# Linear attention: sixteen rows of the output per partition in place of eight, and a second matmul in four blocks of 32 columns

## The chip, the cores and the metric

The kernel runs on one core of a Trainium2 chip. The metric is the device time of one execution in microseconds (us), and the number to forecast is the median of several executions. Before the change the median of three is 126.47 us (126.22 to 126.54).

The names used below: PE is TensorE, which multiplies matrices; PEld is its weight load; DVE is VectorE; ACT is ScalarE; POOL is GpSimd, which here clears a few buffers and issues most of the DMAs; SP is SyncE, which only issues DMAs. SBUF is the on-chip memory of 128 partitions, PSUM the memory that TensorE writes into, DRAM the memory in which inputs and outputs lie.

## The reference

Q, K and V are float32 arrays of 8 x 12 heads, 512 rows and 64 columns. For each of the 96 heads:

```python
Q_feat = np.maximum(0, Q) + 1
K_feat = np.maximum(0, K) + 1
KV = np.einsum('bhkd,bhkv->bhdv', K_feat, V)            # 64 x 64 for a head
K_sum = np.sum(K_feat, axis=2)                          # 64 for a head
numerator = np.einsum('bhqd,bhdv->bhqv', Q_feat, KV)    # 512 x 64
denominator = np.einsum('bhqd,bhd->bhq', Q_feat, K_sum)
out = numerator / (denominator[:, :, :, None] + 1e-10)
```

That is 12.58 MB for each of Q, K, V and the output. The kernel leaves the 1e-10 out, since the denominator is a sum of products that are all at least 1.

## The kernel before

**Heads and groups.** The 96 heads go in twelve groups of eight heads (`NG` = 12), and two groups form a pair `s`, six pairs in all. A DMA load takes a whole pair of one input (1024 KB in SBUF as bf16; POOL's DMAs convert from float32 on the way), except at the start, where K and V come in halves and the first half of Q comes as float32 over SP's queue. K and V are seen as blocks of 128 partitions x 16 rows, so a partition reads 4 KB in one piece from DRAM and a head lies on 32 partitions. Q is seen as blocks of 128 partitions x 32 rows (8 KB in one piece), so a head lies on 16 partitions.

**First matmul.** `k_features` (L150) computes max(x + 1, 1) on DVE. `v_blocks` (L157) copies V into a block-diagonal buffer `v_all`, three of its four 32-partition blocks on DVE (L164) and one on ACT (L162). `keys_values` (L175) then does 32 matmuls of 64 result columns x 260 moving columns a group, with K_sum as an extra column for each head, and ACT moves the result to `kva` (L190, L191), one of `NV` = 4 buffers by group.

**Transposes.** `q_features` (L168) does the same max for Q; `transposes` (L193) turns it with 16 matmuls against an identity, into two PSUM tiles of 1024 columns, and ACT copies each (L204; one of them DVE) to `qt`, in which the columns stand by row-in-block `c`, partition and chunk `r`.

**Second matmul.** `out_matmuls(g, h)` (L206) takes from `qt` 16 partitions x R = 4 chunks, which are 64 columns and so 64 rows of the result, against the 130 columns of a pair of heads in `kva` (numerator and denominator of two heads). Two such blocks (`j`) fill the 128 partitions of PSUM, and eight `c` fill two tiles `o_ps` of two banks each: 16 matmuls a call, two calls a group, 384 in all. `norms` (L223) then takes for each tile a reciprocal of the denominators (L231) and one multiply of 128 x 512 (L232) into `o_sb`. An output partition holds `C` = 8 consecutive rows, which is 2 KB of DRAM. Only two tiles `o_ps` exist, so TensorE refills one while DVE empties the other.

**Order.** The order of the instructions on each engine is the order of the program (`tc.manual_schedule`, L256). In the loop (L275), group `g` is loaded, featured and multiplied while `output(g - 2)` is done two groups later. `load_pair(s + 2)` (L126) is issued by POOL as soon as DVE and ACT have read the buffers of pair `s` (`in_pool` has two of each). No store is issued until all loads are: from `g == NG - 5` on (L290) POOL issues the stores of the groups that are done, one of 1024 KB for each group, and the last two groups are stored over SP's queue, group 10 with one DMA (L138) and group 11 with two halves (L141), of which each takes what one call of `norms(11, h)` has written.

Of the kernel before, what the change touches and what calls it, by code (L numbers as in the profile page):

```python
# [8 lines left out]
FP32 = mybir.dt.float32  # L9
BF16 = mybir.dt.bfloat16  # L10
# [9 lines left out]
def kernel(  # L20
# [19 lines left out]
    nc = tc.nc  # L40

    B, H, S, D = Q.shape
    P = 128
    C = 8
    C2 = 2 * C
    C4 = 4 * C
    R = 4
    NPAIR = B * H * S // (P * C)
    NP = 4
    NG = NPAIR // NP  # L50
    D1 = D + 1
    W = 2 * D1

    def view(t, c):
        return t.flatten_outer_dims().rearrange("(n p c) d -> p n c d", p=P, c=c)

    q_eights = view(Q, C4)
    k_dram = view(K, C2)
    v_dram = view(V, C2)
    o_dram = view(out, C)  # L60

    const = ctx.enter_context(tc.tile_pool(name="const", bufs=1))
    in_pool = ctx.enter_context(tc.tile_pool(name="in_pool", bufs=IN_BUFS))
    kf_pool = ctx.enter_context(tc.tile_pool(name="kf_pool", bufs=2))
    qf_pool = ctx.enter_context(tc.tile_pool(name="qf_pool", bufs=3))
    mid_pool = ctx.enter_context(tc.tile_pool(name="mid", bufs=2))
    out_pool = ctx.enter_context(tc.tile_pool(name="out_pool", bufs=OUT_BUFS))
# [3 lines left out]
    psum_qt = ctx.enter_context(tc.tile_pool(name="psum_qt", bufs=2, space=bass.MemoryType.PSUM))  # L71

    identity = const.tile([P, P], BF16, name="identity")
    NV = 4
    v_all = const.tile([P, 2, 2, C2, 4 * D1], BF16, name="v_all")
    ones = const.tile([P, 4], BF16, name="ones")
    zero = const.tile([P, 1], FP32, name="zero")
    kva_all = const.tile([P, NV, 4, 2, D1], BF16, name="kva_all")
    kva_diag = [kva_all[:, i] for i in range(NV)]

    drams = dict(k=k_dram, v=v_dram)
    raw = {}
    bufs = {}
    kfs = {}
    qfs = {}
    qts = {}
    outs = {}
    cells_of = {}

    def load_first_q():  # L90
        t = out_pool.tile([P, 2 * NP, C, D], FP32, name="o_sb")
        half = t[:, 0:NP].rearrange("p n c d -> p (n c) d")
        nc.sync.dma_start(out=half, in_=q_eights[:, 0])
        return half

    def load_rest_q(t):
        u = in_pool.tile([P, 2, C4, D], BF16, name="q_raw")
        nc.gpsimd.dma_start(out=u[:, 1], in_=q_eights[:, 1])
        for e in range(2):
            raw["q", e] = [  # L100
                x.rearrange("p (r c) d -> p r c d", c=C)[:, :, 4 * e : 4 * e + 4]
                for x in (t, u[:, 1])
            ]

    def load(x, groups):
        s = groups[0] // 2
        if groups[0] % 2 == 0 or (x, s) not in bufs:
            bufs[x, s] = in_pool.tile([P, 4, C2, D], BF16, name=f"{x}_raw")
        if len(groups) == 2:
            ms = slice(0, 4)  # L110
            of = slice(4 * s, 4 * s + 4)
        else:
            ms = slice(groups[0] % 2, 4, 2)
            of = slice(4 * s + groups[0] % 2, 4 * s + 4, 2)
        nc.gpsimd.dma_start(out=bufs[x, s][:, ms], in_=drams[x][:, of])  # L115
        for g in groups:
            raw[x, g] = bufs[x, s][:, g % 2 : 4 : 2]

    def load_q(s):
        t = in_pool.tile([P, 2, C4, D], BF16, name="q_raw")  # L120
        nc.gpsimd.dma_start(out=t, in_=q_eights[:, 2 * s : 2 * s + 2])  # L121
        rows = t.rearrange("p n (r c) d -> p n r c d", c=C)
        for e in range(2):
            raw["q", 2 * s + e] = [rows[:, n, :, 4 * e : 4 * e + 4] for n in range(2)]

    def load_pair(s):  # L126
        load("k", (2 * s, 2 * s + 1))
# [1 line left out]
        load_q(s)  # L129

    def store(g):
        s = g // 2
        o_to = o_dram[:, 2 * NP * s : 2 * NP * s + 2 * NP]
        if g < NG - 2:
            nc.gpsimd.dma_start(out=o_to[:, g % 2 : 2 * NP : 2], in_=outs[s][:, g % 2 : 2 * NP : 2])  # L135
            return
        if g == NG - 2:
            nc.sync.dma_start(out=o_to[:, 0 : 2 * NP : 2], in_=outs[s][:, 0 : 2 * NP : 2])  # L138
            return
        for h in range(2):  # L140
            nc.sync.dma_start(  # L141
                out=o_to[:, 2 * h + g % 2 : 2 * NP : NP], in_=outs[s][:, 2 * h + g % 2 : 2 * NP : NP]
            )

    def feature(dst, src):
        nc.vector.tensor_scalar(  # L146
# [2 lines left out]

    def k_features(g):  # L150
        k_raw = raw.pop(("k", g))
        kf = kf_pool.tile([P, C2, 2, D], BF16, name="kf")
        for n in range(2):
            feature(kf[:, :, n], k_raw[:, n])
        kfs[g] = kf
# [12 lines left out]
    def q_features(g):  # L168
        q_raw = raw.pop(("q", g))
        qf = qf_pool.tile([P, R, C // 2, 2, D], BF16, name="qf")  # L170
        for n in range(2):
# [3 lines left out]
    def keys_values(g):  # L175
        kf = kfs.pop(g)
        kva_ps = psum_kva.tile([P, 4 * D1], FP32, name="kva_ps")
        for c in range(C2):
            for n in range(2):
                nc.tensor.matmul(  # L180
                    kva_ps[64 * n : 64 * n + 64],
                    lhsT=kf[:, c, n, :],
                    rhs=v_all[:, g % 2, n, c, :],
                    start=(c == 0),
                    stop=(c == C2 - 1),
                )
        kva = kva_diag[g % NV]
        for n in range(2):
            ps = slice(64 * n, 64 * n + 64)
            nc.scalar.copy(out=kva[ps, :, n, 0:D], in_=kva_ps[ps, 0 : 4 * D].rearrange("p (b d) -> p b d", b=4))  # L190
            nc.scalar.copy(out=kva[ps, :, n, D], in_=kva_ps[ps, 4 * D : 4 * D1])  # L191

    def transposes(g):  # L193
        qf = qfs.pop(g)
        if g % 2 == 0:
            qts[g // 2] = mid_pool.tile([P, C, P, R], BF16, name="qt")
        for half in range(2):
            qt_ps = psum_qt.tile([P, 2, R, P], BF16, name="qt_ps")
            for c in range(2):
                for r in range(R):  # L200
                    nc.tensor.transpose(qt_ps[:, c, r], qf[:, r, 2 * half + c, :, :], identity)  # L201
            copy = nc.vector.tensor_copy if half and g == NG - 2 else nc.scalar.copy
            lo = g % 2 * 4 + 2 * half
            copy(out=qts[g // 2][:, lo : lo + 2], in_=qt_ps.rearrange("p c r q -> p c q r"))  # L204

    def out_matmuls(g, h):  # L206
        qt = qts[g // 2]
        kva = kva_diag[(g // 2 * 2 + h) % NV]
        ops = [psum.tile([P, 2, BANK], FP32, tag="ps", name="o_ps") for _ in range(2)]
        for c in range(C):  # L210
            for j in range(2):
                b = 2 * (g % 2) + j
                q = 16 * (4 * h + b)
                nc.tensor.matmul(  # L214
                    ops[c // 4][64 * j : 64 * j + 64, c // 2 % 2, (c % 2) * W : (c % 2) * W + W],
                    lhsT=qt[:, c, q : q + 16, :],
                    rhs=kva[:, b],
                    start=True,
                    stop=True,
                )  # L220
        cells_of[g, h] = ops

    def norms(g, h):  # L223
        ops = cells_of.pop((g, h))
        if (g % 2, h) == (0, 0):
            outs[g // 2] = out_pool.tile([P, 2 * NP, C, D], FP32, name="o_sb")
        o_sb = outs[g // 2]
        for i in range(2):
            cells = ops[i][:, :, 0 : 2 * W].rearrange("p b (c n x) -> p b c n x", n=2, x=D1)
            recip = recip_pool.tile([P, 2, 2, 2, 1], FP32, name="recip")  # L230
            nc.vector.reciprocal(out=recip, in_=cells[:, :, :, :, D:D1])  # L231
            nc.vector.tensor_tensor(  # L232
                out=o_sb[:, 2 * h + g % 2 : 2 * NP : NP, 4 * i : 4 * i + 4].rearrange(
                    "p n (b c) d -> p b c n d", b=2
                ),
                in0=cells[:, :, :, :, 0:D],
                in1=recip.to_broadcast([P, 2, 2, 2, D]),
                op=ALU.mult,
            )

    def output(g):
        for h in range(2):
            out_matmuls(g, h)
            norms(g, h)

    def clear(i):
        t = v_all[:, i].rearrange("p n c x -> p (n c x)").bitcast(FP32)
        w = t.shape[1] * 5 // 8
        nc.vector.memset(t[:, 0:w], 0.0)  # L249
        nc.scalar.copy(out=t[:, w:], in_=zero.to_broadcast([P, t.shape[1] - w]))  # L250
        nc.vector.tensor_copy(
            out=v_all[:, i, :, :, 4 * D : 4 * D1].rearrange("p n c j -> p (n c) j"),
            in_=ones[:, None, :].to_broadcast([P, 2 * C2, 4]),
        )

    with tc.manual_schedule():  # L256
# [16 lines left out]
        clear(1)  # L273
        last = NG - 1
        for g in range(last - 1):  # L275
# [11 lines left out]
            keys_values(g)  # L287
            if g % 2 and g // 2 + 2 < NG // 2:
                load_pair(g // 2 + 2)
# [55 lines left out]
```

## Time and profile before

| what | us |
|---|---|
| median of the runs | 126.47 |
| the profiled execution, its own time | 126.1 |
| span of that execution, first to last instruction | 124.3 |
| DVE busy in it | 89.6 |
| TensorE matmuls busy | 63.5 |
| ACT busy | 59.6 |
| last instruction of DVE ends | 113.5 |

The 1.8 us between the span and the execution's own time lie before the first and after the last instruction. The profile cuts the span into 40 slices of 3.1 us and gives for each the busy share of each engine in tenths, the granted TensorE clock, the mean busy share of the 16 DMA engines and what they moved. The rate in GB/s counts the bytes as they stand in SBUF, so a load that converts float32 to bf16 moves twice the shown rate on the DRAM side, and a store just the shown rate. A window is a stretch of the span with the same figures. A share above 1 means that a DMA engine had more than one packet in work.

### The profile page before, as it was taken

How to read it: one execution, taken by the hardware profiler on the slowest of the kernel's cores; microseconds unless marked ns; L12 is line 12 of the kernel's file. 1: busy time of each engine (PE TensorE's matmuls, PEld its weight loads, DVE VectorE, ACT ScalarE, POOL GpSimd, SP SyncE). 2: the span in 40 equal slices, each digit the busy share in tenths (PEclk: the TensorE clock that was granted, in tenths of full speed). 3: DMA queues.
4: the chain of work that ended last, by engine and by line, in shares of the span. 5: the costliest groups of instructions: out<-in, count | busy, mean ns of one | idle time of the engine just before them, and what ended most of it. 6: DMA issues, size and time to landing. Idle time of an engine off the chain costs nothing.

```text
span 124.3 us, 2346 instructions
## 1 busy us (share of the span) xinstructions
PE 63.5 (51%) x960; PEld 52.0 (42%) x960; DVE 89.6 (72%) x190; ACT 59.6 (48%) x86; POOL 25.7 (21%) x53
## 2 busy tenths in 40 slices
PE   0000864500593837629775494928964888652000
PEld 0000754400482737418664383816742757521000
DVE  4885744206999989997999989999169999695000
ACT  7505079606019881866539568393577065300000
POOL 6992021200001400222002392202202200200000
PEclk9999999965579999995899769995596579985555
DMA  3999999999999999999999999999999999999994
GB/s 90 327 211 217 205 208 212 214 214 213 208 211 212 215 223 204 211 213 219 209 212 212 213 215 210 216 208 216 219 287 420 420 419 416 406 415 416 415 409 155
DMA packets 11819, 32.13 MB, mean 258 GB/s; under 512 B 544, under 2 KB 544, under 8 KB 11680
## 3 DMA queue, kind: packets, MB, share of 16 engines
q0 software_dynamic: 10592, 28.84, 97.6%
q1 hardware_dynamic: 1216, 3.15, 6.7%
q8 instruction: 7, 0.11, 0.3%
q14 instruction: 4, 0.03, 0.1%
HBM read 37.75 MB, written 12.58 MB: 405 GB/s over the span
## 4 chain that ended last, share of the span: by engine, by line
DMA 40%; DVE 29%; PE 12%; ACT 7%; issue 2%; POOL 1%; POOLq 0%
DMA v_raw<-in_V_dram 40%; DVE o_sb L232 12%; DVE v_all L164 10%; PE kva_ps L180 8%; ACT qt L204 3%; ACT v_all L162 3%; PE qt_ps L201 3%; DVE recip L231 3%; DVE qf L146 2%; DVE kf L146 1%; PE o_ps L214 1%; DVE qt L204 1%; POOL k_raw L115 1%; ACT kva_all L190 1%; ACT kva_all L191 0%
## 5 line engine op out<-in xcount | busy, mean ns | idle before, releaser
L180 PE MATMUL kva_ps<-v_all,kf 128*64 128x260 bf16 x384 | 30.8, 327 | 15.8 <-DVE v_all L164 14.1
L214 PE MATMUL o_ps<-kva_all,qt 128*64 128x130 bf16 x384 | 20.0, 240 | 31.4 <-DVE recip L231 20.4
L232 DVE TENSOR_TENSOR o_sb<-o_ps,recip 128x512 f32<-128x512 f32 x48 | 33.2, 692 | 1.6
L180 PEld LDWEIGHTS <-kf 128*64 128x64 bf16 x384 | 25.5, 134 | 19.4 <-DVE v_all L164 15.1
L164 DVE COPY v_all<-v_raw 32x2048 bf16<-32x2048 bf16 x36 | 25.5, 710 | 10.6 <-DMA v_raw<-in_V_dram 10.2
L214 PEld LDWEIGHTS <-qt 128*64 128x64 bf16 x384 | 14.0, 118 | 36.5 <-issue 18.3
L162 ACT COPY v_all<-v_raw 32x2048 bf16<-32x2048 bf16 x12 | 22.6, 1893 | 11.2 <-DMA v_raw<-in_V_dram 11.0
L204 ACT COPY qt<-qt_ps 128x1024 bf16<-128x1024 bf16 x23 | 22.2, 1015 | 7.6 <-PE qt_ps L201 7.5
L190 ACT CAST kva_all<-kva_ps 64x256 bf16<-64x256 f32 x24 | 8.9, 372 | 28.2 <-PE kva_ps L180 28.1
L201 PE MATMUL qt_ps<-identity,qf 128*128 128x128 bf16 x192 | 15.3, 240 | 1.8 <-ACT qt L204 1.4
L201 PEld LDWEIGHTS <-qf 128*128 128x128 bf16 x192 | 12.8, 108 | 4.4 <-issue 2.9
L115 POOL DMA_DIRECT2D k_raw<-in_K_dram x7 | 5.4, 773 | 40.0 <-DVE kf L146 39.5
L135 POOL DMA_DIRECT2D out_dram<-o_sb x10 | 7.9, 796 | 26.8 <-DVE o_sb L232 8.8
L231 DVE RECIPROCAL recip<-o_ps 128x8 f32<-128x8 f32 x48 | 9.6, 200 | 5.2 <-PE o_ps L214 5.0
L146 DVE TENSOR_SCALAR kf<-k_raw 128x1024 bf16<-128x1024 bf16 x24 | 10.0, 459 | 4.2 <-PE o_ps L214 3.1
L115 POOL DMA_DIRECT2D v_raw<-in_V_dram x7 | 5.3, 757 | 13.5 <-ACT v_all L162 13.5
L146 DVE TENSOR_SCALAR qf<-q_raw 128x1024 bf16<-128x1024 bf16 x22 | 8.0, 420 | 0.0
L249 DVE MEMSET v_all<- 128x2600 f32 x2 | 4.5, 2225 | 1.1 <-issue 1.1
L191 ACT CAST kva_all<-kva_ps 64x4 bf16<-64x4 f32 x24 | 4.0, 168 | 0.0
L121 POOL DMA_DIRECT2D q_raw<-in_Q_dram x5 | 3.5, 706 | 0.0
L250 ACT COPY v_all<-zero 128x1560 f32<-128x1560 f32 x2 | 2.9, 1488 | 0.0
L271 POOL MEMSET kva_all<- 128x130 bf16 x16 | 2.4, 203 | 0.0
(14 smaller groups left out, 6.6 us busy)
## 6 DMA issues: line engine op xcount, KB each, us to landing
out_dram<-o_sb POOLq DMA_DIRECT2D x10, 1024.0 KB, 24.3
k_raw<-in_K_dram POOLq DMA_DIRECT2D x5, 1024.0 KB, 16.8
v_raw<-in_V_dram POOLq DMA_DIRECT2D x5, 1024.0 KB, 18.3
q_raw<-in_Q_dram POOLq DMA_DIRECT2D x5, 1024.0 KB, 22.5
o_sb<-in_Q_dram SPq DMA_DIRECT2D x1, 1024.0 KB, 4.8
k_raw<-in_K_dram POOLq DMA_DIRECT2D x2, 512.0 KB, 9.5
v_raw<-in_V_dram POOLq DMA_DIRECT2D x2, 512.0 KB, 11.2
out_dram<-o_sb SPq DMA_DIRECT2D x1, 1024.0 KB, 10.7
```

Source lines behind the costliest of these rows:

```text
L115: nc.gpsimd.dma_start(out=bufs[x, s][:, ms], in_=drams[x][:, of])
L135: nc.gpsimd.dma_start(out=o_to[:, g % 2 : 2 * NP : 2], in_=outs[s][:, g % 2 : 2 * NP : 2])
L146: nc.vector.tensor_scalar(out=dst, in0=src, scalar1=1.0, scalar2=1.0, op0=ALU.add, op1=ALU.max)
L162: nc.scalar.copy(out=v_all[ps, g % 2, :, :, b * D : b * D + D], in_=v_raw[ps])
L164: nc.vector.tensor_copy(out=v_all[ps, g % 2, :, :, b * D : b * D + D], in_=v_raw[ps])
L180: nc.tensor.matmul(kva_ps[64 * n : 64 * n + 64], lhsT=kf[:, c, n, :], rhs=v_all[:, g % 2, n, c, :], start=(c == 0), stop=(c == C2 - 1),)
L190: nc.scalar.copy(out=kva[ps, :, n, 0:D], in_=kva_ps[ps, 0 : 4 * D].rearrange("p (b d) -> p b d", b=4))
L201: nc.tensor.transpose(qt_ps[:, c, r], qf[:, r, 2 * half + c, :, :], identity)
L204: copy(out=qts[g // 2][:, lo : lo + 2], in_=qt_ps.rearrange("p c r q -> p c q r"))
L214: nc.tensor.matmul(ops[c // 4][64 * j : 64 * j + 64, c // 2 % 2, (c % 2) * W : (c % 2) * W + W], lhsT=qt[:, c, q : q + 16, :], rhs=kva[:, ...
L231: nc.vector.reciprocal(out=recip, in_=cells[:, :, :, :, D:D1])
L232: nc.vector.tensor_tensor(out=o_sb[:, 2 * h + g % 2 : 2 * NP : NP, 4 * i : 4 * i + 4].rearrange("p n (b c) d -> p b c n d", b=2), in0=cell ...
```

## The change

`C` becomes 16 for the output, as it was for K and V, and `R` becomes 2. An output partition then holds sixteen consecutive rows, 4 KB of DRAM, and a head lies on 32 partitions of the output. The columns of `qt` that belong to one partition block are 16 partitions x 2 chunks = 32, so a result block has 32 rows and four blocks (`b`) fill the 128 partitions of PSUM, each placed with an explicit tile position. A call of `out_matmuls` now handles one group and one half of the sixteen rows instead of half the heads of a pair: it has 32 matmuls of 32 columns in place of 16 of 64, and all four blocks multiply with `kva` of their own group `g`. The two calls of `norms` for a group write different rows `c` of the same partitions in place of different blocks. The two stores of group 11 each take one block, so each needs both calls of `norms(11, ...)`. Loads, features, `v_blocks` and `keys_values` stay as they are but for names.

```diff
-    C = 8
-    C2 = 2 * C
-    C4 = 4 * C
-    R = 4
+    C = 16
+    C4 = 2 * C
+    R = 2
...
     def store(g):
-        s = g // 2
-        o_to = o_dram[:, 2 * NP * s : 2 * NP * s + 2 * NP]
+        s, h = g // 2, g % 2
+        o_to = o_dram[:, 4 * s : 4 * s + 4]
         if g < NG - 2:
-            nc.gpsimd.dma_start(out=o_to[:, g % 2 : 2 * NP : 2], in_=outs[s][:, g % 2 : 2 * NP : 2])
+            nc.gpsimd.dma_start(out=o_to[:, h:4:2], in_=outs[s][:, h:4:2])
             return
         if g == NG - 2:
-            nc.sync.dma_start(out=o_to[:, 0 : 2 * NP : 2], in_=outs[s][:, 0 : 2 * NP : 2])
+            nc.sync.dma_start(out=o_to[:, 0:4:2], in_=outs[s][:, 0:4:2])
             return
-        for h in range(2):
-            nc.sync.dma_start(
-                out=o_to[:, 2 * h + g % 2 : 2 * NP : NP], in_=outs[s][:, 2 * h + g % 2 : 2 * NP : NP]
-            )
+        for n in range(2):
+            nc.sync.dma_start(out=o_to[:, 2 * n + h], in_=outs[s][:, 2 * n + h])
...
     def transposes(g):
...
         for half in range(2):
-            qt_ps = psum_qt.tile([P, 2, R, P], BF16, name="qt_ps")
-            for c in range(2):
+            qt_ps = psum_qt.tile([P, 4, R, P], BF16, name="qt_ps")
+            for c in range(4):
                 for r in range(R):
-                    nc.tensor.transpose(qt_ps[:, c, r], qf[:, r, 2 * half + c, :, :], identity)
+                    nc.tensor.transpose(qt_ps[:, c, r], qf[:, r, 4 * half + c, :, :], identity)
...
-    def out_matmuls(g, h):
+    def out_matmuls(g, half):
         qt = qts[g // 2]
-        kva = kva_diag[(g // 2 * 2 + h) % NV]
+        kva = kva_diag[g % NV]
         ops = [psum.tile([P, 2, BANK], FP32, tag="ps", name="o_ps") for _ in range(2)]
-        for c in range(C):
-            for j in range(2):
-                b = 2 * (g % 2) + j
-                q = 16 * (4 * h + b)
+        for c in range(8):
+            for b in range(4):
+                q = 16 * (4 * (g % 2) + b)
                 nc.tensor.matmul(
-                    ops[c // 4][64 * j : 64 * j + 64, c // 2 % 2, (c % 2) * W : (c % 2) * W + W],
-                    lhsT=qt[:, c, q : q + 16, :],
+                    ops[c // 4][32 * b : 32 * b + 32, c // 2 % 2, (c % 2) * W : (c % 2) * W + W],
+                    lhsT=qt[:, 8 * half + c, q : q + 16, :],
                     rhs=kva[:, b],
                     start=True,
                     stop=True,
+                    tile_position=(0, 32 * b),
                 )
...
-    def norms(g, h):
+    def norms(g, half):
...
+            lo = 8 * half + 4 * i
             nc.vector.tensor_tensor(
-                out=o_sb[:, 2 * h + g % 2 : 2 * NP : NP, 4 * i : 4 * i + 4].rearrange(
-                    "p n (b c) d -> p b c n d", b=2
-                ),
+                out=o_sb[:, g % 2 : 4 : 2, lo : lo + 4].rearrange("p n (b c) d -> p b c n d", b=2),
...
```

More of the change, by code (lines that the diff above doesn't have):

```diff
@@ L43 @@
     P = 128
-    C = 8
-    C2 = 2 * C
-    C4 = 4 * C
-    R = 4
-    NPAIR = B * H * S // (P * C)
-    NP = 4
-    NG = NPAIR // NP
+    C = 16
+    C4 = 2 * C
+    R = 2
+    NQUAD = B * H * S // (P * C)
+    NG = NQUAD // 2
     D1 = D + 1
@@ L57 @@
     q_eights = view(Q, C4)
-    k_dram = view(K, C2)
-    v_dram = view(V, C2)
+    k_dram = view(K, C)
+    v_dram = view(V, C)
     o_dram = view(out, C)
@@ L74 @@
     NV = 4
-    v_all = const.tile([P, 2, 2, C2, 4 * D1], BF16, name="v_all")
+    v_all = const.tile([P, 2, 2, C, 4 * D1], BF16, name="v_all")
     ones = const.tile([P, 4], BF16, name="ones")
@@ L90, in load_first_q @@
     def load_first_q():
-        t = out_pool.tile([P, 2 * NP, C, D], FP32, name="o_sb")
-        half = t[:, 0:NP].rearrange("p n c d -> p (n c) d")
+        t = out_pool.tile([P, 4, C, D], FP32, name="o_sb")
+        half = t[:, 0:2].rearrange("p n c d -> p (n c) d")
         nc.sync.dma_start(out=half, in_=q_eights[:, 0])
@@ L100, in load_rest_q @@
             raw["q", e] = [
-                x.rearrange("p (r c) d -> p r c d", c=C)[:, :, 4 * e : 4 * e + 4]
+                x.rearrange("p (r c) d -> p r c d", c=C)[:, :, 8 * e : 8 * e + 8]
                 for x in (t, u[:, 1])
@@ L107, in load @@
         if groups[0] % 2 == 0 or (x, s) not in bufs:
-            bufs[x, s] = in_pool.tile([P, 4, C2, D], BF16, name=f"{x}_raw")
+            bufs[x, s] = in_pool.tile([P, 4, C, D], BF16, name=f"{x}_raw")
         if len(groups) == 2:
@@ L123, in load_q @@
         for e in range(2):
-            raw["q", 2 * s + e] = [rows[:, n, :, 4 * e : 4 * e + 4] for n in range(2)]
+            raw["q", 2 * s + e] = [rows[:, n, :, 8 * e : 8 * e + 8] for n in range(2)]
     def load_pair(s):
@@ L151, in k_features @@
         k_raw = raw.pop(("k", g))
-        kf = kf_pool.tile([P, C2, 2, D], BF16, name="kf")
+        kf = kf_pool.tile([P, C, 2, D], BF16, name="kf")
         for n in range(2):
@@ L177, in keys_values @@
         kva_ps = psum_kva.tile([P, 4 * D1], FP32, name="kva_ps")
-        for c in range(C2):
+        for c in range(C):
             for n in range(2):
@@ L184, in keys_values @@
                     start=(c == 0),
-                    stop=(c == C2 - 1),
+                    stop=(c == C - 1),
                 )
@@ L197, in transposes @@
         for half in range(2):
-            qt_ps = psum_qt.tile([P, 2, R, P], BF16, name="qt_ps")
-            for c in range(2):
+            qt_ps = psum_qt.tile([P, 4, R, P], BF16, name="qt_ps")
+            for c in range(4):
                 for r in range(R):
-                    nc.tensor.transpose(qt_ps[:, c, r], qf[:, r, 2 * half + c, :, :], identity)
+                    nc.tensor.transpose(qt_ps[:, c, r], qf[:, r, 4 * half + c, :, :], identity)
             copy = nc.vector.tensor_copy if half and g == NG - 2 else nc.scalar.copy
-            lo = g % 2 * 4 + 2 * half
-            copy(out=qts[g // 2][:, lo : lo + 2], in_=qt_ps.rearrange("p c r q -> p c q r"))
-    def out_matmuls(g, h):
+            lo = g % 2 * 8 + 4 * half
+            copy(out=qts[g // 2][:, lo : lo + 4], in_=qt_ps.rearrange("p c r q -> p c q r"))
+    def out_matmuls(g, half):
         qt = qts[g // 2]
-        kva = kva_diag[(g // 2 * 2 + h) % NV]
+        kva = kva_diag[g % NV]
         ops = [psum.tile([P, 2, BANK], FP32, tag="ps", name="o_ps") for _ in range(2)]
-        for c in range(C):
-            for j in range(2):
-                b = 2 * (g % 2) + j
-                q = 16 * (4 * h + b)
+        for c in range(8):
+            for b in range(4):
+                q = 16 * (4 * (g % 2) + b)
                 nc.tensor.matmul(
-                    ops[c // 4][64 * j : 64 * j + 64, c // 2 % 2, (c % 2) * W : (c % 2) * W + W],
-                    lhsT=qt[:, c, q : q + 16, :],
+                    ops[c // 4][32 * b : 32 * b + 32, c // 2 % 2, (c % 2) * W : (c % 2) * W + W],
+                    lhsT=qt[:, 8 * half + c, q : q + 16, :],
                     rhs=kva[:, b],
@@ L219, in out_matmuls @@
                     stop=True,
+                    tile_position=(0, 32 * b),
                 )
-        cells_of[g, h] = ops
-    def norms(g, h):
-        ops = cells_of.pop((g, h))
-        if (g % 2, h) == (0, 0):
-            outs[g // 2] = out_pool.tile([P, 2 * NP, C, D], FP32, name="o_sb")
+        cells_of[g, half] = ops
+    def norms(g, half):
+        ops = cells_of.pop((g, half))
+        if (g % 2, half) == (0, 0):
+            outs[g // 2] = out_pool.tile([P, 4, C, D], FP32, name="o_sb")
         o_sb = outs[g // 2]
@@ L241, in output @@
     def output(g):
-        for h in range(2):
-            out_matmuls(g, h)
-            norms(g, h)
+        for half in range(2):
+            out_matmuls(g, half)
+            norms(g, half)
     def clear(i):
@@ L252, in clear @@
             out=v_all[:, i, :, :, 4 * D : 4 * D1].rearrange("p n c j -> p (n c) j"),
-            in_=ones[:, None, :].to_broadcast([P, 2 * C2, 4]),
+            in_=ones[:, None, :].to_broadcast([P, 2 * C, 4]),
         )
```

## The prediction

> **What bounds the kernel now.** I read the slices first, because they tell whether one resource is full all the time.
>
> ```profile
> DVE  4885744206999989997999989999169999695000
> PEclk9999999965579999995899769995596579985555
> DMA  3999999999999999999999999999999999999994
> GB/s 90 327 211 217 205 208 212 214 214 213 208 211 212 215 223 204 211 213 219 209 212 212 213 215 210 216 208 216 219 287 420 420 419 416 406 415 416 415 409 155
> DMA packets 11819, 32.13 MB, mean 258 GB/s; under 512 B 544, under 2 KB 544, under 8 KB 11680
> q0 software_dynamic: 10592, 28.84, 97.6%
> q1 hardware_dynamic: 1216, 3.15, 6.7%
> q8 instruction: 7, 0.11, 0.3%
> HBM read 37.75 MB, written 12.58 MB: 405 GB/s over the span
> ```
>
> The DMA row is full from the second slice to the last but one. First come the loads (about 212 GB/s counted in bf16, twice that read from DRAM), then from slice 30 on only stores, at about 415. DVE, the busiest engine, has its last work at 113.5 us (the last multiply L232 starts at 112.85 and takes 0.69), and the DMA engines go on for 9 us more. So the span is the time in which 50.3 MB pass the DMA engines, and an edit to compute counts only if it makes them run dry.
>
> Next I asked the windows for stretches with only one kind of transfer. The columns are the stretch, its length, the busy time of PE, PEld, DVE, ACT and POOL with instructions, the clock, the DMA share and GB/s. The first five are K and V loads, the next two POOL's stores, the last SP's stores alone.
>
> ```profile
> 14.00:25.00 11.00, 6.69 (x104) 5.76 (x100) 4.30 (x9) 7.51 (x13) 2.21 (x3) 1.00 1.12 211
> 34.00:42.00 8.00, 5.72 (x91) 4.70 (x88) 7.77 (x19) 4.75 (x8) 0.94 (x2) 0.88 1.12 212
> 48.00:55.50 7.50, 4.09 (x80) 3.42 (x76) 7.34 (x17) 4.70 (x7) 1.13 (x2) 1.00 1.12 212
> 63.00:71.00 8.00, 4.65 (x83) 3.80 (x81) 7.80 (x18) 5.05 (x8) 1.28 (x2) 0.94 1.12 211
> 78.50:85.50 7.00, 4.08 (x75) 3.30 (x70) 6.80 (x17) 4.70 (x7) 1.51 (x2) 0.87 1.13 213
> 94.00:104.00 10.00, 7.52 (x90) 5.54 (x91) 9.82 (x19) 3.70 (x7) 1.35 (x2) 0.66 1.02 419
> 104.00:113.50 9.50, 5.87 (x104) 4.49 (x103) 8.00 (x20) 2.63 (x6) 0.75 (x1) 0.87 1.02 413
> 120.00:121.50 1.50, 0.00 (x0) 0.00 (x0) 0.00 (x0) 0.00 (x0) 0.00 (x0) 0.50 1.05 406
> ```
>
> K and V, read from DRAM in pieces of 4 KB, run at 211.8 on the mean, 423.6 GB/s on the DRAM side. Stores in pieces of 2 KB run at 416.1 from POOL (419 and 413 weighted by length) and at 406 from SP. Q, in pieces of 8 KB, shows 216, 216 and 215 in three shorter stretches (28 to 31, 57 to 61, 73 to 75.5 us): 431 on the DRAM side. The longer the piece, the higher the rate.
>
> Last, the timeline shows what TensorE and DVE do with one output tile, at full clock and (from 111 us) at half clock.
>
> ```profile
> 106.29 0.62 PE L214 MATMUL o_ps<-kva_all,qt 128*64 128x130 bf16 x16
> 108.56 0.42 PE L214 MATMUL o_ps<-kva_all,qt 128*64 128x130 bf16 x8 [0.33 <-DVE o_sb L232]
> 109.26 0.20 DVE L231 RECIPROCAL recip<-o_ps 128x8 f32<-128x8 f32 x1
> 109.49 0.69 DVE L232 TENSOR_TENSOR o_sb<-o_ps,recip 128x512 f32<-128x512 f32 x1
> 111.08 0.65 PE L214 MATMUL o_ps<-kva_all,qt 128*64 128x130 bf16 x8 [0.42 <-DVE o_sb L232]
> ```
>
> Eight matmuls take 0.42 us, sixteen 0.62: eight more cost 0.20, that is 0.05 for each two. DVE needs 0.84 a tile (from one reciprocal's start, 109.26, to the next, 110.10).
>
> **The change part by part.**
>
> *Stores in pieces of 4 KB.* This is the only part on the path that sets the end. Before, POOL stores 10 x 1.05 = 10.49 MB and SP 2.10 MB. POOL: 10.49 MB at 416.1 is 25.20 us; at 423.6, the nearest row with 4 KB on the DRAM side, 24.76: 0.44 saved. SP: 2.10 MB at 406 is 5.17; at 423.6 it is 4.96: 0.21 saved. Sum -0.65 us. Bounds: nothing saved if DRAM's piece is not what sets the rate, and at the rate of the 8 KB loads (431) 0.87 + 0.30 = 1.17 saved. A loss has no row: every longer piece here runs faster. I take -0.65, since 4 KB is the size that comes, though these rows are reads and the change concerns writes.
>
> The Trainium skill, "DMA: Bandwidth & Descriptors", section "Why small descriptors are slow (HBM only)", gives a fixed overhead of about 3 cycles per packet on beats of 32 bytes. Taken per piece, that is an estimate of 2 x 67 = 134 cycles for two 2 KB pieces against 131 for one of 4 KB, so 2.2% of 30 us, 0.7 us, as the rows say. But the section counts packets and says that grouping descriptors into one packet amortizes it; the first rival below works out what that would mean here.
>
> *Twice the matmuls in `out_matmuls`.* 384 matmuls and 384 weight loads more. A tile gets 16 matmuls of 32 columns in place of 8 of 64. If four blocks run side by side as two do now, a tile stays at 0.42 us (0.65 at half clock): no cost, the lower end. If only two run side by side, the row of sixteen gives 0.62, and at half clock about 1.09: the single matmul's 0.32 there leaves 0.33 for three more pairs in the 0.65, so 0.11 a pair, and 0.32 + 7 x 0.11. If none do, 0.22 + 15 x 0.05 = 1.0 and 0.32 + 15 x 0.11 = 2.0, the upper end. I take the first, nearest to the row of two side by side. At up to 0.84 a tile DVE hides it. What hides the rest is the DMA backlog. On the load side, K loads land 16.8 us after issue (median), while 2.1 MB at 424 take 5.0 and some 2.2 are latency (SP's first Q load: 1.05 MB, 2.6 us at 406, landed after 4.8): 9.6 us of others' data lie ahead, and a buffer could come free that much later before the engines run dry. V (18.3) and Q (22.5) have more.
>
> *The backlog at the end.* The last two stores land 10.1 us after issue. Together they are 1.05 MB, which alone would take 4.8 by the same SP row. So about 5 us of lateness of DVE are free; I allow for only 2.5, since SP's first load ran without others beside it.
>
> *The last store waits for both halves.* Before, its first half was issued at 111.89, now both come after the last multiply, 113.54. SP has nothing behind them but the final wait. This takes 1.7 us from the first half's slack, not from the second's, and POOL's queue and store 10 still hold data: 0. If that cover were gone, it would cost half of 1.05 MB, 1.3 us.
>
> *Waits.* `out_matmuls` of an even group no longer needs the next group's `kva`, and its first call needs only its own group's `qt`. In the program's order TensorE still stands behind `keys_values` of the next group (chain: 1.91 us of L180 ahead of L214 at 106.46), so nothing starts earlier: 0. `store(9)` on POOL waited 8.8 us for L232 with store 8's data behind it in the queue; that stays.
>
> *Change of block width.* `keys_values` keeps 64 columns and L214 goes to 32, so TensorE changes shape between them. The nearest row is from transposes (128) to L180: L180 starts 0.07 us before the transposes' last end, while L214 starts 0.17 before L180's end. So about 0.1 us a change; two of them are on DVE's chain (before groups 8 and 10), 0.2 us, hidden by the backlog.
>
> *`qt` copies.* Still 1024 columns each from the same strided read (ACT 1.01 us, DVE 1.22); only the stride's inner run is 2 and not 4. I take 0. If one took twice as long, four a pair would add 4 us to ACT's 10 of each 14.8 us pair (59.6 us over six): still hidden. Features, L231, L232 and the loads keep their sizes.
>
> *Program size.* 768 instructions on top of 2346, while 0.11 MB of instructions are loaded now: 0.04 MB more or, if TensorE alone is what is loaded (1920 instructions), 0.05; at 424 GB/s 0.1 us of DMA. +0.1.
>
> **Sum.** -0.65 + 0.1 = -0.55 us. The profiled execution took 126.1 (span 124.3 and 1.8 around), so its like would take 125.55. It is 0.37 under the median of the runs; from the median the forecast is 126.47 - 0.55 = 125.9 us.
>
> **The rivals.**
>
> *Only the packet counts, not the piece.* From the queue rows: q0's 10592 packets hold K and V (12.58 MB in 2 KB of bf16: 6144) and Q (5.77 MB in 4 KB: 1408); 3040 are left for 10.49 MB and the small ones, so most of POOL's stores are already packets of 4 KB, two pieces each. SP's 1216 are 128 of Q, 1024 of 2 KB and small ones. If so, POOL gains nothing, and SP goes from 406 to 416.1: 5.17 - 5.04 = 0.13 saved, 0.1 lost: 126.4, no change. For it: that count. Against it: K and V go in packets of 2 KB as counted and are still faster than POOL's stores.
>
> *TensorE sets DVE's pace (the other side).* If no 32-column blocks overlap, a tile takes 1.0 us in place of 0.42 and is over DVE's 0.84. From 73.5 us on, where the chain leaves the loads, DVE empties 24 tiles (six groups): 24 x 0.16 = 3.8, and about 0.6 for the first tile of each of six groups, 3.6; at full clock DVE ends 7.4 us later. Less the 5 of backlog that is +2.4, less 0.55: 128.3 us; with eight tiles at half clock 1.0 us each on top, 136. It decides as soon as DVE's end is later than 116 to 118.5. For it: the trace has no 32-column matmul. Against it: two blocks of 64 do overlap. In between, two at a time, tiles at half clock cost 0.25 each and first tiles 0.2: 8 x 0.25 + 6 x 0.2 = 3.2 us, which lies within the backlog of 5 but not of 2.5: 125.9 to 126.6.
>
> The Trainium skill, "TensorE: Matmul & The Clock Gate", section "Wait — 56ns, not 53.3ns?", has matmuls start no closer than about 25 ns. By it, as an estimate, sixteen take 0.38 + 0.22 = 0.6 us at full clock, the same as two at a time. The trace agrees on the mean (0.20 us for eight, 25 ns each), but with 64-column blocks that could as well be the stream of 130 columns.
>
> **How the numbers follow.** Chances: the rate rises with the piece (forecast) 0.65; only packets count 0.20; TensorE's pace, or another loss at the end of the kernel, 0.15. The predicted time is that of the first, 125.9; its own range is 125.3 (431 GB/s) to 126.4 (nothing saved at the stores). A measurement of this kernel tells about 0.3%, 0.38 us, from no change. Within the first case, -0.55 clears that bound by little: 0.50 faster, 0.12 same, 0.03 slower. Packets only: 0.05 faster, 0.13 same, 0.02 slower. The last case: 0.15 slower. Together 0.55, 0.25 and 0.20. The range goes from 125.2 (1.17 saved) to 127.0, which takes in two blocks at a time and leaves out the case of 128 and more.
>
> **What would show it.** Right: GB/s in the store slices at 421 to 426 in place of 415, SP's packets down by 512, L232 ending at 113 to 115, eight L231-L232 steps of 0.84 at the end, and L214 at x16 in about 0.42 us. Wrong: store slices at 416 (packets), or gaps between L231s above 0.84 with L214 as releaser, and DMA slices below 9 ahead of the last (TensorE). Slices of loads that fall below 9 would show that the backlog was smaller than I worked out.

## The result and the profile after

The changed kernel takes 128.3 us (median; 127.98 to 128.53) against 126.47: a ratio of 1.014 with a 95% interval of 1.010 to 1.018. Forecast were 125.9 and a range of 125.2 to 127.0, so the direction and the size are both wrong. The profiled execution took 128.46, with a span of 126.7 against 124.3: 2.4 us more. In the runs further down, four executions that took over 1.5% longer than the fastest of their kernel, one with 192 small matmuls and three with 384, are left out of the medians and ratios.

From the page of the changed kernel, the slices and the queues:

```profile
GB/s 96 319 212 211 211 210 213 211 217 211 208 212 215 215 210 214 209 214 219 208 213 212 218 215 207 213 211 217 226 379 422 418 413 422 415 410 427 416 263 8
DMA packets 11310, 32.18 MB, mean 254 GB/s; under 512 B 544, under 2 KB 544, under 8 KB 11168
q0 software_dynamic: 10592, 28.84, 95.8%
q1 hardware_dynamic: 704, 3.15, 6.2%
q8 instruction: 10, 0.16, 0.5%
```

POOL's queue q0 has the same 10592 packets as before: its stores were packets of 4 KB already, and two pieces of 2 KB have become one. SP's queue q1 has 512 packets fewer. The instruction queue q8 has 10 packets where there were 7. And the last two slices hold 263 and 8 GB/s: the kernel does not run slower throughout, it ends badly.

The windows of the changed kernel, the stretches of the prediction with stores alone and then the end in steps of 1 us (columns as there):

```profile
94.00:104.00 10.00, 7.50 (x120) 5.43 (x121) 9.80 (x21) 3.65 (x7) 1.42 (x2) 0.66 1.02 417
104.00:113.50 9.50, 5.97 (x168) 4.33 (x167) 7.88 (x21) 2.75 (x6) 0.70 (x1) 0.88 1.02 416
122.00:123.00 1.00, 0.00 (x0) 0.00 (x0) 0.00 (x0) 0.00 (x0) 0.00 (x0) 0.50 0.41 168
123.00:124.00 1.00, 0.00 (x0) 0.00 (x0) 0.00 (x0) 0.00 (x0) 0.00 (x0) 0.50 0.13 53
124.00:125.00 1.00, 0.00 (x0) 0.00 (x0) 0.00 (x0) 0.00 (x0) 0.00 (x0) 0.50 0.00 0
125.00:126.70 1.70, 0.00 (x0) 0.00 (x0) 0.00 (x0) 0.00 (x0) 0.00 (x0) 0.50 0.00 0
```

The end of the kernel before, in windows of the same length:

```profile
122.00:123.00 1.00, 0.00 (x0) 0.00 (x0) 0.00 (x0) 0.00 (x0) 0.00 (x0) 0.50 0.52 203
123.00:124.30 1.30, 0.00 (x0) 0.00 (x0) 0.00 (x0) 0.00 (x0) 0.00 (x0) 0.50 0.00 0
```

POOL's stores run at 416.5 GB/s (417 and 416 by length), where they ran at 416.1. From 123 to 124 us a share of 0.13 is two of the sixteen DMA engines still at work; before, all were done at 123. After that nothing at all moves for 2 us and more, where it was 1.3.

The timeline of the changed kernel shows what TensorE and DVE do:

```profile
109.71 0.26 PEld L209 LDWEIGHTS <-qt 128*32 128x32 bf16 x16 [0.57 <-PE o_ps L209]
109.74 0.41 PE L209 MATMUL o_ps<-kva_all,qt 128*32 128x130 bf16 x16 [0.43 <-DVE recip L227]
112.17 0.62 PE L209 MATMUL o_ps<-kva_all,qt 128*32 128x130 bf16 x16 [0.22 <-DVE o_sb L229]
113.11 0.69 DVE L229 TENSOR_TENSOR o_sb<-o_ps,recip 128x512 f32<-128x512 f32 x1
```

Sixteen matmuls of 32 columns take 0.41 us at full clock and 0.62 at half, as eight of 64 did (0.42 and 0.65). DVE's last multiply ends at 113.80 in place of 113.54. Compute is not where the 2.4 us are.

They are at the end, and the trace has an event for each DMA engine that has finished its sixteenth of a DMA. From these events, worked out for some DMAs of both kernels (the sixteen landings, in us after the first of them):

```
before, K load after 0 instruction loads:  0 .. 0.56 (all sixteen)
before, V load after 1:                    0 .. 0.71 (fifteen), 1.55
before, Q load after 2:                    0 .. 0.72 (fourteen), 1.55 1.58
before, V load after 3:                    0 .. 0.65 (thirteen), 1.50 1.54 1.55
before, store after 6:                     0 .. 0.42 (ten), 1.25 1.28 1.31 1.33 1.35 1.36
before, last store, after 7:               0 .. 0.44 (seven), 0.98 1.15 (two), 1.29 .. 1.44 (seven)
after,  store after 8 instruction loads:   0 .. 1.58 (all sixteen)
after,  store after 9:                     0 .. 1.45 (fifteen), 2.82
after,  last store, after 10:              0 .. 1.46 (fourteen), 2.50 2.71
```

Each instruction load of 16 KB, a single packet of 0.88 to 1.09 us in the traces, makes one DMA engine late by about 1.1 us, and it stays late while data is queued behind it, since every DMA gives each engine its share. As long as each load falls on another engine, the slowest engine is one load late, however many loads there are. The landings of the changed kernel read so up to the eighth load; after the ninth, one engine is two steps behind, and after the tenth two are, as if these loads had fallen on engines that were late already.

The second part is POOL. Its last instruction before the final barrier is a drain of its DMA queue. From the same trace:

```
                                    before   after
POOL's last store has landed        120.61  124.67
POOL's drain ends                   121.89  125.94
SP's last store has landed          123.44  124.49
last instruction of the span        124.33  126.69
```

The drain ends 1.27 us after POOL's last landing. Before, that was over when SP's last store landed; now POOL's store lands last and the drain is in the open. In these two traces the parts add up to the 2.4 us: SP's last store lands 1.05 us later, and the span ends 2.20 us after that landing, where it was 0.89.

### The profile page after: what moved, and what is told of

Same layout as the page of the kernel before. It is cut to its first block, busy times and chain, and to the rows that moved or that the text cites. A ratio compares the mean times of both kernels' runs of the same rounds, so it can differ in the third digit from the quotient of the medians.

```text
span 126.7 us, 3115 instructions
## 1 busy us (share of the span) xinstructions
PE 64.0 (51%) x1344; PEld 50.6 (40%) x1344; DVE 89.0 (70%) x190; ACT 59.6 (47%) x86; POOL 25.1 (20%) x53
## 3 DMA queue, kind: packets, MB, share of 16 engines
q0 software_dynamic: 10592, 28.84, 95.8%
## 4 chain that ended last, share of the span: by engine, by line
DMA 39%; DVE 28%; PE 12%; ACT 7%; issue 2%; POOL 1%; POOLq 0%
DMA v_raw<-in_V_dram 39%; DVE o_sb L229 12%; DVE v_all L160 10%; PE kva_ps L176 8%; ACT qt L200 3%; ACT v_all L158 3%; PE qt_ps L197 3%; DVE recip L227 3%; DVE qf L142 2%; PE o_ps L209 1%; DVE kf L142 1%; DVE qt L200 1%; POOL k_raw L113 1%; ACT kva_all L186 1%; ACT kva_all L187 0%
## 5 line engine op out<-in xcount | busy, mean ns | idle before, releaser
L209 PE MATMUL o_ps<-kva_all,qt 128*32 128x130 bf16 x768 | 19.8, 238 | 31.4 <-DVE recip L227 17.8
L209 PEld LDWEIGHTS <-qt 128*32 128x32 bf16 x768 | 12.7, 102 | 37.9 <-DVE o_sb L229 16.1
L133 POOL DMA_DIRECT2D out_dram<-o_sb x10 | 7.3, 738 | 27.3 <-DVE recip L227 9.1
L142 DVE TENSOR_SCALAR kf<-k_raw 128x1024 bf16<-128x1024 bf16 x24 | 9.4, 433 | 4.2 <-PE kva_ps L176 3.0
## 6 DMA issues: line engine op xcount, KB each, us to landing
out_dram<-o_sb POOLq DMA_DIRECT2D x10, 1024.0 KB, 24.8
```

The source lines that it names most:

```text
L133: nc.gpsimd.dma_start(out=o_to[:, h:4:2], in_=outs[s][:, h:4:2])
L142: nc.vector.tensor_scalar(out=dst, in0=src, scalar1=1.0, scalar2=1.0, op0=ALU.add, op1=ALU.max)
L209: nc.tensor.matmul(ops[c // 4][32 * b : 32 * b + 32, c // 2 % 2, (c % 2) * W : (c % 2) * W + W], lhsT=qt[:, 8 * half + c, q : q + 16, :], ...
```

## The experiments

The theories: **I**, the longer program of TensorE loads more instructions, and late DMA engines set the end; **P**, SP's packets of 4 KB take more of the engines' turns, so POOL's last store lands last and its drain is exposed; **S**, the 4 KB pieces themselves cost the time; **M**, the 32-column blocks slow TensorE or DVE. The ratios below are to the kernel before, which was run beside them: 126.3 us with the first four, 126.39 with the next four, 126.33 with the last.

### The matmul's half alone (m32_only)

The kernel before, with:

```diff
-            for j in range(2):
-                b = 2 * (g % 2) + j
-                q = 16 * (4 * h + b)
+            for i in range(4):
+                b = 2 * (g % 2) + i // 2
+                q = 16 * (4 * h + b) + 8 * (i % 2)
...
-                    ops[c // 4][64 * j : 64 * j + 64, c // 2 % 2, (c % 2) * W : (c % 2) * W + W],
-                    lhsT=qt[:, c, q : q + 16, :],
+                    ops[c // 4][32 * i : 32 * i + 32, c // 2 % 2, (c % 2) * W : (c % 2) * W + W],
+                    lhsT=qt[:, c, q : q + 8, :],
...
+                    tile_position=(0, 32 * i),
```

> The kernel before with the second matmul alone in four blocks of 32 columns; the output keeps eight rows a partition and its stores their 2 KB pieces. Theory I (instruction loads): TensorE's program grows by 768 instructions, so 10 loads of 16 KB in place of 7; each holds one DMA engine for some 0.6 to 0.9 us, the ninth and tenth hit engines that were already late, and the end waits for the slowest engine: 127.4 to 127.9 us, with 10 instruction packets. Theory S (the 4 KB pieces of the stores cost the time): 126.5. Theory P (only SP's larger packets cost it, by making POOL's last store land last): 126.5.

Measured: 127.63 us, ratio 1.0085 (1.0057 to 1.0112). Its queue row and the end of its windows:

```profile
q8 instruction: 10, 0.16, 0.5%
```

```profile
122.00:123.00 1.00, 0.00 (x0) 0.00 (x0) 0.00 (x0) 0.00 (x0) 0.00 (x0) 0.50 0.54 207
123.00:124.00 1.00, 0.00 (x0) 0.00 (x0) 0.00 (x0) 0.00 (x0) 0.00 (x0) 0.50 0.13 51
124.00:125.50 1.50, 0.00 (x0) 0.00 (x0) 0.00 (x0) 0.00 (x0) 0.00 (x0) 0.50 0.02 7
```

Two engines are at work between 123 and 124 us, as in the changed kernel, with no 4 KB piece in any store. In the last store fourteen engines land by 123.33 and two at 124.61 and 124.62. POOL's last store lands at 122.34, its drain ends at 123.61 and is covered. Theory I alone, 1.3 us.

### The stores' half alone (s4k_cols64)

The changed kernel, with:

```diff
-            for b in range(4):
+            for j in range(2):
+                b = 2 * j
...
-                    ops[c // 4][32 * b : 32 * b + 32, c // 2 % 2, (c % 2) * W : (c % 2) * W + W],
-                    lhsT=qt[:, 8 * half + c, q : q + 16, :],
+                    ops[c // 4][64 * j : 64 * j + 64, c // 2 % 2, (c % 2) * W : (c % 2) * W + W],
+                    lhsT=qt[:, 8 * half + c, q : q + 32, :],
...
-                    tile_position=(0, 32 * b),
```

> The changed kernel with its second matmul in 16 matmuls of 64 columns a call in place of 32 of 32. It leaves out part of the computation: of each two neighbouring blocks of heads, the second is multiplied with the first one's kva. All stores stay at 4 KB pieces. Theory I: 7 instruction loads, no late engine, 126.2 to 126.6 us. Theory S: still 128.3. Theory P without theory I: POOL's drain stays exposed, about 127.3.

Measured: 127.19 us, ratio 1.0064 (1.0034 to 1.0095). The end of its windows:

```profile
122.00:123.00 1.00, 0.00 (x0) 0.00 (x0) 0.00 (x0) 0.00 (x0) 0.00 (x0) 0.50 0.35 139
123.00:124.00 1.00, 0.00 (x0) 0.00 (x0) 0.00 (x0) 0.00 (x0) 0.00 (x0) 0.50 0.00 0
124.00:125.40 1.40, 0.00 (x0) 0.00 (x0) 0.00 (x0) 0.00 (x0) 0.00 (x0) 0.50 0.00 0
```

With 7 loads no engine is at work after 123, yet the span goes on for 2.4 us. POOL's last store lands at 123.40 (120.61 before), SP's at 123.20, and the drain ends at 124.67. That is the number expected for P without I: P costs 0.9 us by itself. S is out for the whole 1.8, since the same stores in the changed kernel go with 128.3.

### SP's pieces back to 2 KB (sp_pieces_2k)

The changed kernel, with:

```diff
-            nc.sync.dma_start(out=o_to[:, 0:4:2], in_=outs[s][:, 0:4:2])
+            for i in range(2):
+                cs = slice(8 * i, 8 * i + 8)
+                nc.sync.dma_start(out=o_to[:, 0:4:2, cs], in_=outs[s][:, 0:4:2, cs])
...
-        for n in range(2):
-            nc.sync.dma_start(out=o_to[:, 2 * n + h], in_=outs[s][:, 2 * n + h])
+        for i in range(2):
+            cs = slice(8 * i, 8 * i + 8)
+            nc.sync.dma_start(out=o_to[:, h:4:2, cs], in_=outs[s][:, h:4:2, cs])
```

> The changed kernel with SP's stores (groups 10 and 11) in pieces of 2 KB, two DMAs by halves of the sixteen rows each. Theory I: the late engine stays, but SP's packets of 2 KB leave POOL two thirds of each engine, so POOL's last store lands before SP's and its drain is hidden: 127.2 to 127.6, 10 instruction packets. Theory P alone: 126.4. Theory S with POOL's pieces as cause: 128.3.

Measured: 127.5 us, ratio 1.0094 (1.0056 to 1.0133). POOL's last store lands at 123.45 in place of 124.67, SP's at 124.65, and the drain ends at 124.72, just covered. The late engines stay: two at 124.59 and 124.65, the others by 123.48. P is removed, I is left, in this execution and by the median. But three of the nine executions took 128.36 to 128.58, as long as the changed kernel; what made them longer is not shown.

### Fewer instructions elsewhere (few_instr)

The changed kernel, with:

```diff
-        for c in range(C):
-            for n in range(2):
+        for n in range(2):
...
-                    lhsT=kf[:, c, n, :],
-                    rhs=v_all[:, g % 2, n, c, :],
+                    lhsT=kf[:, 0, n, :],
+                    rhs=v_all[:, g % 2, n, 0, :],
```

> The changed kernel, second matmul and stores untouched, with the first matmul cut to the first of its sixteen rows a partition (30 of 32 matmuls a group left out, so KV and K_sum are sums over a sixteenth of the rows). TensorE's program is 720 instructions shorter. Theory I: 7 instruction loads, no late engine, 126.0 to 126.5 us. Theory S: 128.3. Theory P without theory I: 127.3. Theory M (32-column blocks themselves slow TensorE or DVE): 128 or more, as the second matmul stays.

Measured: 127.96 us (126.97 to 128.76), ratio 1.0102 (1.0052 to 1.0152), which meets no theory's number. It settles little. TensorE's program came out at 8 loads, not the 7 expected (1989 records in the trace). The profiled execution took 126.97, with no engine of POOL's last store two steps behind, and the exposed drain (POOL's last landing 123.17, drain until 124.44, last instruction 125.2), which is P alone. But the runs spread over 1.8 us, and TensorE, with little to do, had a granted clock of 0.66 to 0.77; in two runs the time is 2.3 and 3.0 us over the span, where it is 1.8 to 2.1 in the others. The reason was not followed up and stays open.

### Instructions alone: 96, 192 and 384 small matmuls (pad96, pad192, pad384)

The kernel before, with this ahead of the first matmul and n as each expectation has it:

```diff
         kva_ps = psum_kva.tile([P, 4 * D1], FP32, name="kva_ps")
+        for _ in range(n.get(g, 0)):
+            nc.tensor.matmul(
+                kva_ps[0:64, 0:8],
+                lhsT=identity[:, 0:64],
+                rhs=identity[:, 0:8],
+                start=True,
+                stop=True,
+            )
```

> The kernel before with 96 small matmuls more (8 columns of the identity, overwritten before use) ahead of the first matmul of group 2, where TensorE waits for V anyway; nothing else. TensorE's program grows by 192 instructions, so 8 instruction loads. Theory I with engines taken in turn from eight: no engine is hit twice, no change, 126.1 to 126.5 us. If every further load costs at the end: about 126.7. If 32-column blocks and not the program's length are the cause: 126.3.

> As the run with 96, with 192 small matmuls (64 ahead of group 0, 128 ahead of group 2): 384 instructions more, 9 instruction loads. Theory I: the ninth load hits an engine that is late already, the end moves by one load's delay, 0.9 to 1.3 us: 127.2 to 127.6 if one engine late is enough. If only the 32-column blocks cost: 126.3.

> As the run with 96, with 384 small matmuls (64, 128 and 32 ahead of each of groups 3 to 8): 768 instructions more, the same number as the changed kernel has, 10 instruction loads. Theory I: as with 9 loads, two engines late by the same amount: 127.2 to 127.8. If only the 32-column blocks cost: 126.3, or a little more for TensorE's longer work.

Measured: 126.37 (ratio 0.9996, 0.9962 to 1.0029) with 8 loads; 127.47 (1.0072, 1.004 to 1.0103) with 9; 127.62 (1.0092, 1.0055 to 1.013; 127.18 to 128.58) with 10. The end of the windows with 384:

```profile
122.00:123.00 1.00, 0.00 (x0) 0.00 (x0) 0.00 (x0) 0.00 (x0) 0.00 (x0) 0.50 0.68 262
123.00:124.00 1.00, 0.00 (x0) 0.00 (x0) 0.00 (x0) 0.00 (x0) 0.00 (x0) 0.50 0.27 104
124.00:125.00 1.00, 0.00 (x0) 0.00 (x0) 0.00 (x0) 0.00 (x0) 0.00 (x0) 0.50 0.07 27
```

Stores and matmul shapes are those of the kernel before, and still a step is there: no change with eight loads, 1.1 us with nine, 1.2 with ten, where the times spread most. With ten it is about that of m32_only (1.3), so M is not needed for it. Here four engines land at 124.61 to 124.74 and twelve by 123.45, so the loads are not dealt out strictly in turn. The executions agree: with 7 and 8 loads most take 126.0 to 126.6 us, but some 126.9 to 127.5, as if two loads had met on one engine; the profile of the run with 96 matmuls is one of these (127.41, one engine at 124.77 and fifteen by 123.79). With 9 loads none is below 127.09.

The run with 96 shows one thing more. The small matmuls took longer than TensorE's wait for V, and DVE's last multiply ended at 118.41, 4.9 us later than before, with no change of the median. In the run with 192 it ended at 120.38, 6.8 us later, and there the DMA engines ran dry:

```profile
117.00:118.00 1.00, 0.51 (x10) 0.34 (x12) 0.94 (x4) 0.00 (x0) 0.00 (x0) 0.98 0.71 277
```

In its last store no engine is two steps behind: fourteen land within 0.43 us of each other, up to 123.86, and two one step later, at 124.70 and 124.82. So the 1.1 us of this run mix a dry spell with the ninth load, and it does not show that the ninth load made an engine late twice. The evidence for that is m32_only and the run with 384, whose DVE ends at 115.15, within what costs nothing, and whose engines never ran dry (share of 1.01 or more in every stretch up to 122 us).

### Both causes removed (s4k_cols64_sp2k)

The edits of s4k_cols64 and sp_pieces_2k together.

> The changed kernel with 64-column matmuls (the second of each two blocks is multiplied with the first one's kva, so part of the computation is left out) and with SP's stores in pieces of 2 KB. POOL's stores keep their 4 KB pieces. If the time is made of instruction loads and of POOL's exposed drain alone, both are gone here: 126.1 to 126.5. If POOL's 4 KB pieces cost or gain anything, it shows as the difference to 126.3.

Measured: 126.2 us, ratio 0.9977 (0.9948 to 1.0006). The whole loss is gone, and POOL's ten stores in pieces of 4 KB are worth nothing that can be told from zero. Its windows with mostly POOL's stores:

```profile
94.00:104.00 10.00, 7.30 (x100) 5.64 (x98) 9.76 (x21) 3.86 (x8) 1.52 (x2) 0.83 1.02 420
104.00:113.50 9.50, 4.79 (x90) 3.57 (x84) 7.03 (x17) 1.55 (x5) 0.70 (x1) 0.81 1.02 414
```

The rate is 417.1 by length, against 416.1: 0.06 us on 25. The four corners fit together: 126.2 with neither cause, 127.19 with P, 127.63 and 127.5 with I, 128.3 with both. P's 0.9 to 1.0 and I's 1.2 to 1.3 add up to a little more than the 1.8 to 2.0 of both together.

This run and s4k_cols64 differ in SP's stores alone. SP's last one lands at 123.30 here and at 123.20 with pieces of 4 KB, so SP is not slower with these; POOL's last store lands at 121.72 here and at 123.40 there, although SP's stores start sooner here (first packet at 110.98 against 112.57).

### Store 9 on SP (store9_sp)

The changed kernel, with:

```diff
-        if g < NG - 2:
+        if g < NG - 3:
...
-        if g == NG - 2:
-            nc.sync.dma_start(out=o_to[:, 0:4:2], in_=outs[s][:, 0:4:2])
+        if g < NG - 1:
+            nc.sync.dma_start(out=o_to[:, h:4:2], in_=outs[s][:, h:4:2])
```

> The changed kernel with the store of group 9 issued by SP in place of POOL; every piece stays at 4 KB and the second matmul at 32 columns. POOL's last store is then that of group 8, which lands some microseconds before the end. Theory P as POOL's drain after its last landing (1.27 us): the drain is hidden, 127.2 to 127.6, the same as with SP's stores in pieces of 2 KB. If SP's 4 KB pieces cost time themselves: 128.3 or more.

Measured: 128.25 us, ratio 1.0132 (1.009 to 1.0173): a miss. POOL's last store is now that of group 8, but it still lands last, at 124.79, and the drain ends at 126.02, 1.23 us later. Its SP and POOL timelines say why: SP issues store 9 at 103.37, ahead of what POOL still has queued, and from then on takes its turns on every engine.

```profile
103.37 5.11 SPq L136 DMA_DIRECT2D out_dram<-o_sb  x2
111.46 0.85 SPq L139 DMA_DIRECT2D out_dram<-o_sb  x2
```

```profile
96.63 0.93 POOL L133 DMA_DIRECT2D out_dram<-o_sb  x1 [1.84 <-DMA out_dram<-o_sb]
```

POOL's last store, issued at 96.63, needs 28 us to land (24.8 is the median of POOL's stores in the changed kernel). The link between POOL's last landing and the end holds again; what I had wrong is that fewer stores on POOL would end sooner. The run by itself does not exclude that SP's 4 KB pieces cost something directly; the two runs with 64-column matmuls do, since SP's last store lands no later there with pieces of 4 KB (123.20 against 123.30).

None of the kernels beats the one before.

## Why the prediction was wrong, point by point

*What bounds the kernel.* Right: the DMA engines set the end and compute does not. But I took them as one resource with one rate. The end is that of the slowest of sixteen engines and of the queue that drains last, and the mean share of the slices hides both until the last two slices.

*Stores in pieces of 4 KB, -0.65.* This is the first step that failed. The gain of 0.44 on POOL's stores is not there (416.5 against 416.1 GB/s; 126.2 against 126.39 in the run with both causes removed). My row was K and V against POOL's stores, which differ in direction and conversion as well as in length. My first rival had it: POOL's packets were 4 KB already, and 416 in the store slices was my own sign for it. The section of the Trainium skill that I cited ("DMA: Bandwidth & Descriptors", "Why small descriptors are slow (HBM only)") counts packets, and the trace agrees with that reading: the same 10592 packets, the same rate. For SP, whose packets did grow, the end of the changed kernel has 421 GB/s (116 to 119 us) and 434 (119 to 120), against 412 and 410 in the same windows before, but the span is not set by it.

*Program size, +0.1.* The mechanism was in the sum and its size was wrong by a factor of twelve: 1.2 to 1.3 us. I spread 0.05 MB over all engines. The three loads more cost one engine's time for one load, about 1.1 us, since two of them, as the landings read, fell on engines that were late already.

*The last store waits for both halves, 0, and the arbitration.* Here stood "POOL's queue and store 10 still hold data", and I counted that as cover for SP. I did not ask what is late next on POOL: with SP's packets at 4 KB the engines' turns are shared by half, POOL's last store lands 1.7 us later than with SP's at 2 KB (121.72 to 123.40 in the runs with 64-column matmuls; 123.45 to 124.67, 1.2 us, with 32), and behind it on POOL stands a drain that ends 1.27 us after the landing. That costs 0.9 us and was in no rival; only the chances left room for "another loss at the end of the kernel".

*The sum, -0.55.* With what was measured it is 0 for POOL's stores, +1.2 to 1.3 for the program and +0.9 to 1.0 for the drain, in place of -0.65, +0.1 and 0.

*Twice the matmuls, 0.* Right: 0.41 us for sixteen. The 25 ns between starts that the Trainium skill gives ("TensorE: Matmul & The Clock Gate", "Wait — 56ns, not 53.3ns?") does not hold between blocks of different columns here: (0.41 - 0.22) / 15 is 13 ns on the mean, and the four blocks of a group mostly start 2 to 5 ns apart. The kernel before shows it already, which I overlooked: its two blocks start 3 to 4 ns apart and the next two 53 to 77 ns later, and my mean of 25 ns hid that.

*The backlog, 5 us.* Right, and safer than I dared to count: DVE ending 4.9 us later changed nothing (126.37); ending 6.8 us later, with 192 small matmuls, it let the engines run dry.

*Waits, block width, `qt` copies.* Right within what the trace can tell: DVE's end moved by 0.26 us in all, the `qt` copies on ACT kept 1.01 us.

*The rivals.* Packets only gave 126.4, right on its mechanism, blind to the end. TensorE's pace gave 128.3, the very time measured, by a mechanism that is not there (0.41 us a tile, DVE's end 0.26 us later): that is luck. The upper end of the range took in bounds of compute and none of the DMA side's own end.

## What to carry to other kernels

Where DMA sets the end, look at each DMA engine's and each queue's own last landing, not at the mean rate: a few instructions more can be free or cost a microsecond, depending on whether an engine is made late twice. Before a store is moved or its packets are resized, ask which queue lands last and what that queue's issuer still has to do after it. And a rate from a row in the other direction is a bound at best; count packets before and after first.

## What the runs showed of the hardware that I had not expected

- TensorE's instructions come in loads of 16 KB: 7 loads for 1940 TensorE records in the trace, 8 for 1989 and 2132, 9 for 2324, 10 for 2708. Each holds one DMA engine and makes it about 1.1 us late for the data queued behind. After the engines had run dry (192 small matmuls) fourteen of them landed within 0.43 us of each other again.
- With eight loads the median did not move, and with ten it rose by 1.2 to 1.3 us (the 1.1 with nine mix in a dry spell); but with ten loads two engines were two steps behind in m32_only and four in the run with 384 small matmuls. What picks the engine stays open: the trace does not name it.
- POOL's drain ended 1.23 to 1.28 us after its last DMA had landed in every kernel above.
- Two queues share an engine by packets: SP's packets at 4 KB in place of 2 delayed POOL's last landing by 1.7 us (64-column matmuls) and 1.2 us (32) with the same bytes in all. The Trainium skill says so ("DMA: Bandwidth & Descriptors", "Queues, rings and completion order": each engine goes round its queues packet by packet), and this agrees.
